# Recurrence of a hybrid transformer block on one core: the order of the next unit's transposes, its decay scan and its matmul bursts

## The chip, the core and the metric

The kernel runs on one core of a Trainium2 chip, in one launch. Five engines work side by side, each in the order of its own instruction queue: PE (matrix products, into PSUM), DVE (elementwise work), ACT (activations and copies), POOL (a few elementwise operations and some transfers) and SP (which here issues most of the DMA transfers). An instruction that waits for a semaphore holds everything behind it on its engine. The metric is the device time of one execution in microseconds; lower is better. One execution was recorded by the profiler.

## What is computed

One block with batch 1, 1024 tokens, width 1024. Two mixers read the same normalised input: an attention with a forget gate (8 heads of 64) and a linear recurrence of the RWKV-7 kind (8 heads of 64). Both are gated, added, projected, and followed by a convolutional feed-forward network. The recurrence, which is what the change touches:

```python
def step(state, inp):
    r_t, w_t, k_t, v_t, a_t, b_t = inp
    sa = jnp.einsum('bhvk,bhk->bhv', state, a_t)
    state = state * w_t[:, :, None, :] + sa[..., None] * b_t[:, :, None, :] \
        + v_t[..., None] * k_t[:, :, None, :]
    y_t = jnp.einsum('bhvk,bhk->bhv', state, r_t)
    return state, y_t
```

`w_t` is the decay `exp(-exp(w_log))`, and `a_t`, `b_t` come from the normalised key. The rest, in short:

```python
u = modulate(rms_norm(h, ln1_g), shift1, scale1)
p_fox, p_rwkv, p_gate = split(u @ w_in)
merged = sigmoid(gate_fox) * (o_fox @ fox_w_out) + sigmoid(gate_rwkv) * (o_rwkv @ rwkv_w_out)
h = h + gate1 * (merged @ w_o)
h = h + gate2 * conv_ffn(modulate(rms_norm(h, ln2_g), shift2, scale2))
return rms_norm(h, final_g)
```

## The kernel before

**Stages.** Load and normalise the input; small projections; the recurrence (about 180 to 665 us of the recorded span); the attention (to about 876 us); the merge, the output projection and the feed-forward network. Large products are made with operands split in a high and a low part (`hi`, `lo`), each a 128x128 weight tile against 512 columns.

**Units of the recurrence.** The heads are taken in four pairs `p`, the tokens in two halves `hf` of 512: eight units, numbered `k`, in the order (0,0), (0,1), (1,0) and so on. A unit has 8 chunks of 64 tokens. Its work falls in two generators.

`pre(k, p, hf)` prepares a unit. On DVE the decay scan `cum` (line 728) runs over the loaded decays; ACT makes the exponentials `el` and `en` from it; DVE makes `ar` and `bk` (lines 744 to 760) out of them. The PE burst `p` (two times 16 small matmuls, `bk` against `ar`) gives the chunk matrices `E` (DVE, line 776). They go out to DRAM (`sm`) and come back in another layout (`M`, four loads). On DVE 31 steps of two instructions each (`t`, line 796, and `E`, line 798; here called the inverse) invert the 32x32 blocks; step `s` is 31-s columns wide. The result goes out again (`se`) and comes back as `TT`. Meanwhile PE does transposes `vt`, `at`, `tb` and the product `q`.

`main(k, p, hf)` runs a unit. DVE transposes the blocks of `TT` into `X` (two instructions, line 853), PE does the small products `xi` and `zi` that complete the inverse, then `uw` and `mz` with DVE copies `Wt`, `Zt`, `Mt` between them, and then the scan over the 8 chunks: at each chunk PE adds to `sp` and `yp`, and DVE makes the new state `S` from `sp` (line 916), which the next chunk's PE step needs. At the end come the group norm of the output (`mu`, `va`) and the write `d_orw`.

**What sets the order.** PE's order is written out by the class `Weave`, a planner with its own clock `now`, in ns. Each matmul adds a fixed cost to it. A generator that yields a number asks to be resumed that much later. `run` resumes whichever chain is due, spawned chains (0) ahead of `main` (1) ahead of `pre` (2); while none is due, `fill` emits the next matmuls of the large projections: q and k (`qk`), r, k and v of the next head pair (`ps_rkv`), attention's values (`v`), and 16 gates (`gt`), of 48 matmuls each. Gates that are left when the recurrence ends are emitted in the same way in the attention, into the one bank `rk_ps`. `ready` is the planned time at which `TT` is expected: `main` does not emit `xi` before it. DVE, ACT, POOL and SP are ordered in this stage by the framework's scheduler, which works from priorities and its own estimates; a manual dependency of the kind `NOSYNC` only forbids it to place one instruction of an engine ahead of another.

Of the kernel before, what the change touches and what calls it, by code (L numbers as in the profile page):

```python
# [12 lines left out]
ALU = mybir.AluOpType  # L13
# [22 lines left out]
NOSYNC = mybir.DependencyInfo(mybir.DependencyClass.NoSync, mybir.DependencyReason.DATA)  # L36
# [11 lines left out]
class Weave:  # L48
# [27 lines left out]
    def add(self, load, run):  # L76
        self.queue.append((load, run))

    def prefetch(self):
        while (self.first or self.queue) and len(self.loaded) < 1:  # L80
            load, run = (self.first or self.queue).popleft()
            self.loaded.append((load(), run))
# [30 lines left out]

        self.live.append([self.now + wait, 0, chain])

    def run(self, chains):

        self.live = [[self.now, 1 + i, g] for i, g in enumerate(chains)]
        while self.live:
            due = min((c for c in self.live if c[0] <= self.now), key=lambda c: (c[1], c[0]), default=None)  # L120
            if due is None:
                self.fill(min(c[0] for c in self.live))
                continue
            wait = next(due[2], None)
            if wait is None:
                self.live.remove(due)
            else:
                due[0] = self.now + max(wait, 0.0)
# [3 lines left out]
def hybrid_block(ctx: ExitStack, tc: tile.TileContext, a, out):  # L132
    nc = tc.nc
    weave = Weave()
    ctx.enter_context(tc.manual_schedule(engines={mybir.EngineType.PE}))

    def mm(o, lhsT, rhs, start, stop, more=False):

        weave.mm_cost(o, lhsT, rhs)
        nc.tensor.matmul(o, lhsT, rhs, start=start, stop=stop, skip_group_check=more)  # L140
# [8 lines left out]
    tt, stt, ts = nc.vector.tensor_tensor, nc.vector.scalar_tensor_tensor, nc.vector.tensor_scalar  # L149
# [19 lines left out]
    def C(name):  # L169
        o, k = CST[name]  # L170
        return cst[:, o : o + k] if o < NC1 else cst2[:, o - NC1 : o - NC1 + k]
# [163 lines left out]
    with ExitStack() as es:  # L335
# [26 lines left out]
        def rkv_items(p, hf):  # L362
            ts_ = {x: rkp.tile([128, NH], F32, tag=f"{x}{hf}", name=f"{x}{p}{hf}") for x in "rkv"}
            rkv[p, hf], got[p, hf] = [ts_[x] for x in "rkv"], 0

            def steps(w, x, t):
                if hf == 0:
                    last_col[p, x] = shp.tile([128, 1], F32, tag=f"pv{x}", name=f"pv{p}{x}")
                yield from shifted(w, t, hf, ts_[x], last_col[p, x], f"rkv{t}")
                got[p, hf] += 1  # L370

            for x, t in (("k", 4 + p), ("r", p), ("v", 8 + p)):
                yield (lambda t=t: w_in(12 + t)), (lambda w, x=x, t=t: steps(w, x, t))
# [322 lines left out]
            return ap.rearrange("p (c x) -> p c x", x=x)  # L696

        BKS = (slice(0, 2), slice(1, 3))
        state, units, passed = {}, {}, set()

        blk_r = rw.tile([128, 128], F32R, name="blk_r")
        nc.scalar.copy(blk_r, C("blk"))
# [9 lines left out]
        def pre(k, p, hf):  # L712
# [5 lines left out]
            def tmp(nm, w=NH, bufs=1, dt=F32):  # L718
                return rw.tile([128, w], dt, tag=nm, name=f"{nm}{n}", bufs=bufs)

            def chunk_tile(nm, bufs, *dims):
                return rw.tile([128, *dims], F32, tag=nm, name=f"{nm}{n}", bufs=bufs)

            cum = tmp("cum")
            nc.sync.dma_start(cum, d_lora[0, p, :, cs])
            al = tmp("al")
            nc.sync.dma_start(al, d_lora[1, p, :, cs])
            nc.vector.tensor_tensor_scan(cum, C("reset"), cum, initial=0.0, op0=ALU.mult, op1=ALU.add)
            el = chunk_tile("el", 1, NCU, CH + 1)
            nc.gpsimd.memset(el[:, :, 0:1], 1.0)  # L730
            nc.scalar.activation(el[:, :, 1:], c3(cum), AF.Exp, scale=-DEC)
# [25 lines left out]
            pcd = chunk_tile("pcd", 3, NCU)  # L757
# [28 lines left out]
            M32 = chunk_tile("M32", 1, 32, 32)  # L786
            for g in range(4):
                nc.sync.dma_start(M32[g * 32 : g * 32 + 32, :, :], sm.rearrange("h c b s t -> (h c b) s t"))
            ready = weave.now + (46000 if k == 0 else 38500)
            E32 = chunk_tile("E32", 1, 8, 32)  # L790
            nc.gpsimd.tensor_copy(E32, C("einit").rearrange("p (j t) -> p j t", t=32))
            t32 = tmp("t32", 256)
            for s in range(31):
                J, W = s // 4 + 1, 31 - s
                tv = t32[:, 0 : J * W].rearrange("p (j w) -> p j w", w=W)
                tt(tv, E32[:, 0:J, s : s + 1].to_broadcast([128, J, W]),  # L796
                   M32[:, s : s + 1, s + 1 : 32].to_broadcast([128, J, W]), op=ALU.mult)
                tt(E32[:, 0:J, s + 1 : 32], E32[:, 0:J, s + 1 : 32], tv, op=ALU.add)  # L798
            se = scr.tile([2, NCU, 2, 32, 32], F32, tag="se", name=f"se{n}")
            for g in range(4):  # L800
                nc.sync.dma_start(
# [2 lines left out]
            TT = chunk_tile("TT", 2, NCU, CH)  # L804
# [37 lines left out]
        def main(k, p, hf):  # L842
# [3 lines left out]
            pcd, ar, E, QA, TT, bon, UV = (o[k] for k in ("pcd", "ar", "E", "QA", "TT", "bon", "UV"))  # L846


            X = rw.tile([128, NCU, 32], F32, tag="X", name=f"X{n}", bufs=1)
            B0 = (slice(0, 32), slice(64, 96))  # L850
            B1 = (slice(32, 64), slice(96, 128))
            for h in range(2):
                nc.vector.transpose(X[B0[h], :, :], TT[B0[h], :, 0:32])
            yield max(0, o["ready"] - weave.now)
            xi = gen(f"xi{n}")
            for c in range(NCU):
# [39 lines left out]
            sp = py.tile([128, NCU, CH], F32, tag="sp", name=f"sp{n}")  # L896
            S0 = state.get(p)

            def fixed(c):

                alone = hf == 0 and c == 0
                for h in range(2):
                    mm(sp[HS[h], c, :], E[:, c, h, 2, :], UV[:, c, h, :], start=True, stop=alone)
                for h in range(2):
                    mm(yp[HS[h], c, :], UV[:, c, h, :], E[:, c, h, 1, :], start=True, stop=alone)
# [3 lines left out]
            for c in range(NCU):  # L909
                if S0 is not None:  # L910
                    for h in range(2):
                        mm(sp[HS[h], c, :], Mt[HS[h], c, :], S0[HS[h], :], start=False, stop=True)
                S1 = None
                if not (hf == 1 and c == NCU - 1):
                    S1 = rw.tile([128, CH], F32, tag="state", name=f"S{n}{c}", bufs=3)
                    ts(S1, sp[:, c, :], pcd[:, c : c + 1], None, op0=ALU.mult)
                if S0 is not None:
                    for h in range(2):
                        mm(yp[HS[h], c, :], S0[HS[h], :], Zt[HS[h], c, :], start=False, stop=True)
                if c + 1 < NCU:  # L920
                    yield 1150
                    fixed(c + 1)
                S0 = state[p] = S1
# [55 lines left out]
        def pre_chain():  # L979
            for k, (p, hf) in enumerate(order):  # L980
                while got[p, hf] < 3:
                    weave.step()
                yield from pre(k, p, hf)
                if p < 3:
                    weave.first.extend(rkv_items(p + 1, hf))
                yield 0

        def main_chain():
            for k, (p, hf) in enumerate(order):
                while (p, hf) not in units:  # L990
                    yield 200
                yield from main(k, p, hf)
                yield 0

        weave.run([main_chain(), pre_chain()])
    rk_st.close()


# [307 lines left out]
    for x in range(2):  # L1306
        for n in range(8):
            if x or n:
                k = 8 * x + n + 1
# [157 lines left out]
    due = []  # L1467
# [248 lines left out]
    units = [(k, j) for k in ORDER for j in range(NP)]  # L1716
# [265 lines left out]
```

## Time and profile before

| | us |
|---|---|
| median of 3 runs | 1717.37 |
| the runs | 1715.96, 1721.29, 1717.37 |
| span of the profiled execution | 1713.2 |
| mean granted PE clock over the span | 0.986 |

The profile records the span from the first to the last instruction of the profiled execution and no other time of it; the runs' median is 4.2 us above that span.

The views used: the page's summary; the waits by engine (who sat idle for whom, in total us, number of times, longest); the timeline (start, duration, engine, line, operation, output<-inputs, shapes, count, and in brackets the idle time just before with what ended it); windows (busy time of each engine in a stretch, then the granted PE clock as a share of full speed, the DMA engines' share and GB/s); the DMA issues with the time to landing. A few stretches of this kernel, from windows of 100 us:

| stretch, us | PE busy | DVE busy | PE clock |
|---|---|---|---|
| 200 to 300 | 96.89 | 80.56 | 0.98 |
| 300 to 400 | 96.66 | 75.15 | 1.00 |
| 400 to 500 | 95.28 | 72.56 | 0.98 |
| 500 to 600 | 96.54 | 70.52 | 0.98 |
| 600 to 700 | 96.21 | 37.38 | 0.98 |
| 800 to 900 | 94.70 | 79.34 | 1.00 |
| 1000 to 1100 | 99.98 | 58.14 | 1.00 |

### The profile page before, as it was taken

Reading aid. Unit: us, or ns where it says so; the run is one execution under the profiler, and the core shown is the slowest. Engines: PE = TensorE matmul, PEld = TensorE weight load, DVE = VectorE, ACT = ScalarE, POOL = GpSimd, SP = SyncE. Lnnn points to the kernel's source line nnn. Section 1 sums busy time; section 2 is a strip of 40 time slices with the busy share of each in tenths; the row PEclk is TensorE's granted clock in tenths of the full one; section 3 lists DMA queues with packets and bytes.
Section 4 is the critical chain, followed back from the end, with each engine's and each line's share of the span. In section 5 each row is a group of like instructions: output and inputs, shape, how many; then the busy total and the mean of one; then the engine's idle time right before and its main releaser. Section 6 shows DMA issues by size and latency. Waiting matters only on the chain.

```text
span 1713.2 us, 26506 instructions
## 1 busy us (share of the span) xinstructions
PE 1665.3 (97%) x9984; PEld 1367.0 (80%) x9984; DVE 1213.0 (71%) x2432; ACT 813.1 (47%) x1482; POOL 143.5 (8%) x175
## 2 busy tenths in 40 slices
PE   8899999999999999999999999999999999999998
PEld 7867777787777777888878888888888888888886
DVE  4576687777677632889777734897777777786677
ACT  5364343334344454766652314664444444454455
POOL 0001011111110002323212100000000000000000
PEclk9899999999999999999999999999999999999999
DMA  9287644533333226434268611132333223484463
GB/s 310 89 304 236 185 133 112 140 96 116 95 96 98 85 81 158 135 100 125 75 231 288 255 50 62 57 105 98 106 116 111 93 99 117 149 293 153 123 215 111
DMA packets 135311, 239.87 MB, mean 140 GB/s; under 512 B 39888, under 2 KB 64720, under 8 KB 135184
## 3 DMA queue, kind: packets, MB, share of 16 engines
q1 hardware_dynamic: 127232, 220.94, 39.8%
q0 software_dynamic: 7952, 17.25, 3.7%
q8 instruction: 78, 1.28, 0.3%
q14 instruction: 49, 0.40, 0.1%
HBM read 172.59 MB, written 65.54 MB: 139 GB/s over the span
## 4 chain that ended last, share of the span: by engine, by line
PE 80%; DVE 9%; DMA 4%; ACT 3%; SPq 2%; issue 1%; DVEq 0%; ACTq 0%; POOLq 0%
PE X L140 13%; PE D L140 12%; PE Y L140 6%; PE wo L140 5%; PE gt L140 5%; PE br L140 5%; PE ps_rkv L140 5%; PE qk L140 4%; PE rk_ps L140 4%; PE W L140 3%; PE lg L140 2%; PE ov L140 2%; PE tr L140 2%; PE sp L140 2%; PE tp L144 2%
## 5 line engine op out<-in xcount | busy, mean ns | idle before, releaser
L140 PE MATMUL D<-op,op 128*128 128x512 f32 x924 | 209.8, 389 | 0.0
L140 PEld LDWEIGHTS D<-op,op 128*128 128x128 f32 x924 | 173.3, 188 | 36.3 <-DVE op L1245 0.3
L140 PE MATMUL X<-T_m,S 128*128 128x512 f32 x440 | 107.3, 390 | 0.1
L140 PEld LDWEIGHTS X<-T_m,S 128*128 128x128 f32 x440 | 82.4, 188 | 18.2 <-ACT T_m L1670 0.6
L1244 ACT CAST op<-g 128x512 fp32r<-128x512 f32 x77 | 47.8, 621 | 73.0 <-PE D L140 47.9
L1245 DVE TENSOR_TENSOR op<-g,op 128x512 fp32r<-128x512 f32 x77 | 53.0, 689 | 40.9 <-ACT op L1244 40.8
L1481 DVE SCALAR_TENSOR_TENSOR c<-ab,vec,c 128x512 f32<-128x512 f32 x88 | 65.9, 749 | 19.5 <-ACT c L1484 17.9
L263 DVE TENSOR_TENSOR lo_in<-raw_in,hi_in 128x512 fp32r<-128x512 f32 x84 | 56.4, 706 | 31.6 <-PE gt L140 12.3
L796 DVE TENSOR_TENSOR t<-E,M 128x60 f32<-128x60 f32 (+24 forms) x248 | 56.8, 229 | 29.5 <-DMA M<-sm 24.2
L1445 DVE TENSOR_TENSOR S<-ur,S 128x512 fp32r<-128x512 f32 x66 | 45.5, 691 | 35.6 <-ACT S L1441 35.5
L261 ACT CAST hi_in<-raw_in 128x1024 fp32r<-128x1024 f32 x42 | 43.9, 1047 | 52.5 <-PE ps_rkv L140 17.2
L1441 ACT CAST S<-ur 128x512 fp32r<-128x512 f32 x66 | 41.0, 622 | 55.6 <-DVE ur L1434 30.6
L1445 DVE TENSOR_TENSOR A<-ur,A 128x512 fp32r<-128x512 f32 x64 | 44.0, 688 | 30.9 <-ACT A L1441 30.7
L140 PE MATMUL Y<-T_h,A 128*128 128x512 f32 x264 | 63.5, 389 | 0.0
L140 PE MATMUL Y<-T_h,S 128*128 128x512 f32 x264 | 63.3, 389 | 0.0
L140 PE MATMUL X<-B_b,A 128*128 128x512 f32 x252 | 60.8, 390 | 0.0
L140 PE MATMUL W<-B_f,A 128*128 128x512 f32 x252 | 60.6, 389 | 0.0
L1066 ACT ACTIVATE P<-lg,nm 128x896 f32<-128x896 f32 (+3 forms) x64 | 47.5, 744 | 22.1 <-DVE nm L1062 21.9
L140 PEld LDWEIGHTS Y<-T_h,A 128*128 128x128 f32 x264 | 49.6, 188 | 10.4
L798 DVE TENSOR_TENSOR E<-E,t 128x60 f32<-128x60 f32 (+24 forms) x248 | 53.7, 216 | 5.8
L140 PEld LDWEIGHTS Y<-T_h,S 128*128 128x128 f32 x264 | 49.5, 188 | 10.3
L1441 ACT CAST A<-ur 128x512 fp32r<-128x512 f32 x64 | 39.9, 623 | 34.2 <-PE X L140 31.5
(472 smaller groups left out, 4213.3 us busy)
## 6 DMA issues: line engine op xcount, KB each, us to landing
raw_in<-in_w_in SPq DMA_DIRECT2D x50, 512.0 KB, 3.7
wm<-in_w_mod SPq DMA_DIRECT2D x48, 512.0 KB, 6.5
ur<-in_w_up SPq DMA_DIRECT2D x44, 512.0 KB, 4.0
g<-d_g SPq DMA_DIRECT2D x35, 512.0 KB, 3.9
d_g<-gs SPq DMA_DIRECT2D x44, 256.0 KB, 2.0
d_g<-c SPq DMA_DIRECT2D x33, 256.0 KB, 4.4
d_st<-qh SPq DMA_DIRECT2D x64, 128.0 KB, 2.4
d_gate<-gs SPq DMA_DIRECT2D x32, 256.0 KB, 2.6
```

What stands on the lines that cost most here:

```text
L140: nc.tensor.matmul(o, lhsT, rhs, start=start, stop=stop, skip_group_check=more)
L144: nc.tensor.transpose(o, i, eye)
L261: nc.scalar.copy(hi, raw)
L263: nc.vector.tensor_tensor(lo[:, c : c + NH], raw[:, c : c + NH], f32(hi[:, c : c + NH]), op=ALU.subtract)
L796: tt(tv, E32[:, 0:J, s : s + 1].to_broadcast([128, J, W]), M32[:, s : s + 1, s + 1 : 32].to_broadcast([128, J, W]), op=ALU.mult)
L798: tt(E32[:, 0:J, s + 1 : 32], E32[:, 0:J, s + 1 : 32], tv, op=ALU.add)
L1066: nc.scalar.activation(e[:, 0:n], lg[:, 0:n], AF.Exp, bias=nm[:, 0:1], accum_out=nm[:, 1:2])
L1244: nc.scalar.copy(hi, src)
L1245: tt(lo, src, f32(hi), op=ALU.subtract)
L1441: nc.scalar.copy(hi, src)
L1445: tt(lo, src, f32(hi), op=ALU.subtract)
L1481: stt(c, ab[:, x + hf * NH : x + hf * NH + NH], V("conv_w", 22 * x + i), c, op0=ALU.mult, op1=ALU.add)
```

## The change

It has four parts, all in the recurrence. (1) From the second unit on, the decay scan `cum` may not stand on DVE ahead of step 22 of the inverse of the unit before. (2) From the second unit on, the transposes `X` may not stand on DVE ahead of the last state `S` of the unit before. (3) The first unit's planned `ready` is 6000 ns later. (4) `run` gets `beside` (2600 ns): when a `pre` burst is due, and the next `main` step or spawned chain falls due within 2600 ns, PE is filled up to that step, the step is emitted first, and the burst right behind it.

```diff
-    def run(self, chains):
+    def run(self, chains, beside=0.0):
 
         self.live = [[self.now, 1 + i, g] for i, g in enumerate(chains)]
+        led = False
         while self.live:
             due = min((c for c in self.live if c[0] <= self.now), key=lambda c: (c[1], c[0]), default=None)
-            if due is None:
-                self.fill(min(c[0] for c in self.live))
+            lead = min((c[0] for c in self.live if c[1] < 2), default=None)
+            if due is None or (due[1] > 1 and not led and lead is not None and lead < self.now + beside):
+                self.fill(min(c[0] for c in self.live) if due is None else lead)
+                led = False
                 continue
+            led = beside > 0 and (led or due[1] < 2)
             wait = next(due[2], None)
...
-        state, units, passed = {}, {}, set()
+        state, units, passed, placed = {}, {}, set(), {}
...
-            nc.vector.tensor_tensor_scan(cum, C("reset"), cum, initial=0.0, op0=ALU.mult, op1=ALU.add)
+            i = nc.vector.tensor_tensor_scan(cum, C("reset"), cum, initial=0.0, op0=ALU.mult, op1=ALU.add)
+            if k:
+                tc.add_manual_dep(i.ins, placed["inverse"].ins.name, NOSYNC)
...
-            ready = weave.now + (46000 if k == 0 else 38500)
+            ready = weave.now + (52000 if k == 0 else 38500)
...
-                tt(E32[:, 0:J, s + 1 : 32], E32[:, 0:J, s + 1 : 32], tv, op=ALU.add)
+                i = tt(E32[:, 0:J, s + 1 : 32], E32[:, 0:J, s + 1 : 32], tv, op=ALU.add)
+                if s == 22:
+                    placed["inverse"] = i
...
-                nc.vector.transpose(X[B0[h], :, :], TT[B0[h], :, 0:32])
+                i = nc.vector.transpose(X[B0[h], :, :], TT[B0[h], :, 0:32])
+                if k:
+                    tc.add_manual_dep(i.ins, placed["state"].ins.name, NOSYNC)
...
-                    ts(S1, sp[:, c, :], pcd[:, c : c + 1], None, op0=ALU.mult)
+                    placed["state"] = ts(S1, sp[:, c, :], pcd[:, c : c + 1], None, op0=ALU.mult)
...
-        weave.run([main_chain(), pre_chain()])
+        weave.run([main_chain(), pre_chain()], beside=2600.0)
```

What it does to the engines' orders shows at three places. In the names, the digits behind a tile's name are its unit's half (and the chunk, for `S_11`: half 1, chunk 1) and a buffer number; line numbers of the changed kernel are a few higher.

First, DVE while the first unit (0,0) is being inverted and the second, (0,1), prepared. Before:

```order
L384 SCALAR_TENSOR_TENSOR ql_1_1811<-qk_1_1718,qh_1_1809 128x512
L728 SCALAR_TENSOR_TENSOR cum_1_1792<-cst_120,cum_1_1792 128x512
L798 TENSOR_TENSOR E_0_1607<-E_0_1607,t_0_1609 128x3x23
L796 TENSOR_TENSOR t_0_1609<-E_0_1607,M_0_1602 128x66
L798 TENSOR_TENSOR E_0_1607<-E_0_1607,t_0_1609 128x3x22
L753 TENSOR_TENSOR ar_1_1856<-r_748,el_1_1797 128x512
```

Now:

```order
L267 TENSOR_TENSOR lo_in_1923<-raw_in_1920,hi_in_1922 128x512 x2
L802 TENSOR_TENSOR t_0_1609<-E_0_1607,M_0_1602 128x54
L388 SCALAR_TENSOR_TENSOR ql_1_1912<-qk_1_1885,qh_1_1910 128x512
L804 TENSOR_TENSOR E_0_1607<-E_0_1607,t_0_1609 128x6x9
L732 SCALAR_TENSOR_TENSOR cum_1_1792<-cst_120,cum_1_1792 128x512
L802 TENSOR_TENSOR t_0_1609<-E_0_1607,M_0_1602 128x48
L804 TENSOR_TENSOR E_0_1607<-E_0_1607,t_0_1609 128x6x8
L802 TENSOR_TENSOR t_0_1609<-E_0_1607,M_0_1602 128x49
L804 TENSOR_TENSOR E_0_1607<-E_0_1607,t_0_1609 128x7x7
L755 SCALAR_TENSOR_TENSOR ar_1_1856<-kr_1_1853,nkk,el_1_1797 128x512
```

The scan of (0,1) stood behind the inverse's step 7 (the `E` of 2x24 is some rows above it, that of 3x23 right behind it) and now stands behind step 22 (`E` of 6x9); 29 instructions of the inverse have moved ahead of it. PE's order is the same in both kernels up to and past the burst `p` of (0,1).

Second, DVE in the scan of unit (1,1), with the transposes of (2,0). Before:

```order
L916 TENSOR_SCALAR S_11_4469<-sp_1_4401,pcd_1_3030 128x64
L750 SCALAR_TENSOR_TENSOR kr_1_4411<-kr_1_4411,vec,al_1_4323 128x512
L853 STREAM_TRANSPOSE X_0_4862<-TT_0_4032 32x256
L751 TENSOR_TENSOR bk_1_4413<-kr_1_4411,en_1_4329 128x8x64
L754 TENSOR_SCALAR al_1_4323<-al_1_4323,vec,oka 128x512
L853 STREAM_TRANSPOSE X_0_4862<-TT_0_4032 32x256
L916 TENSOR_SCALAR S_12_4485<-sp_1_4401,pcd_1_3030 128x64
```

Now (all states of the scan stand above these rows):

```order
L804 TENSOR_TENSOR E_0_4143<-E_0_4143,t_0_4145 128x8
L782 TENSOR_TENSOR E_1_4716<-p_2_100_4719,cst_120 128x4x128
L782 TENSOR_TENSOR E_1_4716<-p_2_110_4720,cst_120 128x4x128
L267 TENSOR_TENSOR lo_in_4108<-raw_in_4105,hi_in_4107 128x512 x2
L267 TENSOR_TENSOR lo_in_4748<-raw_in_4745,hi_in_4747 128x512 x2
L861 STREAM_TRANSPOSE X_0_4928<-TT_0_4213 32x256
L978 TENSOR_TENSOR vs_7_4741<-v_7_4686,vs_7_4741 128x4x64
L861 STREAM_TRANSPOSE X_0_4928<-TT_0_4213 32x256
```

The two transposes no longer stand between two states; they stand behind the first half of the next unit's `E`.

Third, PE where the recurrence ends and the attention begins. Before:

```order
L140 MATMUL va_1_6960<-Zts_1_6961,blk_r 128x512
L140 MATMUL va_1_6960<-Mts_1_6962,blk_r 128x512
L140 MATMUL gt_1_6975<-u_lo,hi_in_6792 128x512 x3
L140 MATMUL gt_1_6975<-u_hi,lo_in_6793 128x512 x8
L140 MATMUL rk_ps<-u_hi,hi_in_6928 128x512 x8
L140 MATMUL rk_ps<-u_lo,hi_in_6928 128x512 x8
L140 MATMUL rk_ps<-u_hi,lo_in_6929 128x512 x8
```

Now:

```order
L144 MATMUL va_1_6988<-Zts_1_6989,blk_r 128x512
L144 MATMUL va_1_6988<-Mts_1_6990,blk_r 128x512
L144 MATMUL gt_0_7014<-u_lo,hi_in_6903 128x512 x7
L144 MATMUL gt_0_7014<-u_hi,lo_in_6904 128x512 x8
L144 MATMUL gt_1_7090<-u_hi,hi_in_6903 128x512 x8
L144 MATMUL gt_1_7090<-u_lo,hi_in_6903 128x512 x8
L144 MATMUL gt_1_7090<-u_hi,lo_in_6904 128x512 x8
L144 MATMUL rk_ps<-u_hi,hi_in_7009 128x512 x8
```

One more gate (48 matmuls) is emitted in the recurrence: 10 there and 6 in the attention, where it was 9 and 7. From the last head sums `va` to the attention's first gate there were 11 matmuls and are 39. In the attention the gate matmuls that are missing are those of its last part.

## Prediction

> **What bounds the kernel now.** I read the page's summary first:
>
> ```profile
> span 1713.2 us, 26506 instructions
> PE 1665.3 (97%) x9984; PEld 1367.0 (80%) x9984; DVE 1213.0 (71%) x2432; ACT 813.1 (47%) x1482; POOL 143.5 (8%) x175
> ```
>
> PE is busy for 97% of the span, and the change leaves the set of matmuls as it is: they only change places. So the time can move only by PE's idle time and by stretches in which PE runs at a lower granted clock. The waits of PE say for whom it idles (us in total, times, longest):
>
> ```profile
> PE sp L140 <- DVE S L916: 8.3, 6, 2.5
> ...
> PE rk_ps L140 <- ACT gm L1167: 3.7, 2, 3.5
> ...
> PE xi L140 <- DVE X L853: 3.1, 2, 1.8
> ...
> PE ps_rkv L140 <- DVE k L358: 1.4, 1, 1.4
> PE at L144 <- DVE E L776: 1.1, 1, 1.1
> ```
>
> In the recurrence that is 8.3+3.1+1.4+1.1 = 13.9 us. DVE's timeline shows what DVE stood on just before; the bracket is its own idle time:
>
> ```profile
> 241.70 0.43 DVE L853 STREAM_TRANSPOSE X<-TT 32x256 f32<-32x256 f32 x1 [5.01 <-DMA TT<-se]
> 305.24 1.23 DVE L728 TENSOR_TENSOR_SCAN cum<-cst,cum 128x512 f32<-128x512 f32 x1 [2.10 <-DMA cum<-d_lora]
> 405.21 1.22 DVE L728 TENSOR_TENSOR_SCAN cum<-cst,cum 128x512 f32<-128x512 f32 x1 [2.61 <-DMA cum<-d_lora]
> 432.80 0.43 DVE L853 STREAM_TRANSPOSE X<-TT 32x256 f32<-32x256 f32 x1 [2.79 <-DMA TT<-se]
> 500.07 0.43 DVE L853 STREAM_TRANSPOSE X<-TT 32x256 f32<-32x256 f32 x1 [4.37 <-DMA TT<-se]
> 542.98 0.43 DVE L853 STREAM_TRANSPOSE X<-TT 32x256 f32<-32x256 f32 x1 [3.04 <-DMA TT<-se]
> ```
>
> Each time DVE stands in front of a scan or a transpose whose data has not landed, and a state `S` that is ready to be made waits behind it. PE then stands at `sp`, as in these two:
>
> ```profile
> 435.11 0.34 PE L140 MATMUL sp<-UV,E 128*64 128x64 f32 x4 [2.45 <-DVE S L916]
> 544.30 0.34 PE L140 MATMUL sp<-UV,E 128*64 128x64 f32 x4 [2.23 <-DVE S L916]
> ```
>
> And behind three of the stalls the granted clock (the column after POOL) halves:
>
> ```profile
> 244.50:247.90 3.40, 3.40 (x9) 2.75 (x9) 3.02 (x13) 1.83 (x4) 0.19 (x1) 0.50 0.45 147
> 435.70:439.10 3.40, 3.40 (x18) 2.24 (x16) 2.04 (x4) 0.57 (x1) 0.00 (x0) 0.50 0.20 69
> 544.90:548.30 3.40, 3.40 (x20) 2.24 (x18) 3.13 (x6) 1.25 (x2) 0.00 (x0) 0.50 0.22 80
> ```
>
> Each of these windows is 3.4 us at half speed, so about 1.7 us of work is lost in it, 5.1 in all.
>
> **The stalls that go.** The second part forbids `X` ahead of the last `S`, so the stalls at 435.11 and 544.30 and the one behind 500.07 lose their cause; the first part does the same for `cum` at 305.24 and 405.21. The first unit's transposes (241.70) have no state to wait for. There PE itself stands at `xi` (3.1 us in the waits); the third part lets it do 6 us of other matmuls first, which covers it. Of the 13.9 us I put 0.7 down to ordinary late states that have no such wait on DVE in front: 13.2 go, and with the clock 13.2+5.1 = **-18.3 us**. The bounds are -13.2, if the half-clock windows come anyway, and -18.3.
>
> **The stall that comes.** In the first overlap, unit (0,1) being prepared, DVE has no wait on `cum` that would be worth removing, yet the scan goes behind step 22 of the inverse there too. PE's order is the same up to the burst `p`. Before:
>
> ```profile
> 201.21 0.19 DVE L796 TENSOR_TENSOR t<-E,M 128x31 f32<-128x31 f32 x1 [5.65 <-DMA M<-sm]
> 207.75 1.21 DVE L728 TENSOR_TENSOR_SCAN cum<-cst,cum 128x512 f32<-128x512 f32 x1
> 210.78 0.22 DVE L796 TENSOR_TENSOR t<-E,M 128x60 f32<-128x60 f32 x1
> 211.04 0.22 DVE L798 TENSOR_TENSOR E<-E,t 128x60 f32<-128x60 f32 x1
> 214.72 0.69 DVE L751 TENSOR_TENSOR bk<-kr,en 128x512 f32<-128x512 f32 x1
> 216.66 0.68 DVE L756 TENSOR_TENSOR bk<-al,en 128x512 f32<-128x512 f32 x1
> 218.06 1.28 DVE L263 TENSOR_TENSOR lo_in<-raw_in,hi_in 128x512 fp32r<-128x512 f32 x2
> 219.27 0.68 DVE L384 SCALAR_TENSOR_TENSOR ql<-qk,qh 128x512 fp32r<-128x512 f32 x1
> 218.08 1.16 PE L140 MATMUL p<-ar,bk 64*128 64x128 f32 x16
> ```
>
> The last `bk` ends at 216.66+0.68 = 217.34, and `p` starts at 218.08: there is less than 1 us of slack. Now 29 instructions of the inverse go ahead of `cum`. One takes 0.26 us with its gap (210.78 to 211.04): 7.5 us. With them two `ql`, the pair `lo_in` and one `kr` go ahead: 0.6+0.6+1.2+0.6 (each counted 0.6 because the next starts before the 0.68 are over, as at 218.06 to 219.27, 1.21 for two), less 0.4 of overlap: 10.1 together, so `cum` starts at 217.9 and not 207.75. Behind it come the scan 1.2, four more of the inverse 1.0, seven operations that make `ar` and `bk` (seven times about 0.6 = 4.2) and four more of the inverse that overlap them partly, 0.6. The last `bk` is done at 217.9+1.2+1.0+4.2+0.6 = 224.9. PE stands at `p` from 218.08, for 6.9 us, with all its matmuls and weight loads queued behind. The inverse cannot start earlier to make room: at 201.21 DVE had already idled 5.65 us for `M`. Stalls a third as long were followed by half clock above, so I add 1.3 of the 1.7 (part of that window may fall into the stall itself): **+8.2 us**. The bounds are 6 (overlap as close as it gets, no clock) and 10.
>
> **The later odd units.** When (1,0), (2,0) and (3,0) are inverted, `main` of the unit before runs its scan, and now `cum` and two `lo` fall between two states.
>
> ```profile
> 269.21 0.33 PE L140 MATMUL sp<-S,Mt 64*64 64x64 f32 x4
> 271.56 0.33 PE L140 MATMUL sp<-S,Mt 64*64 64x64 f32 x4
> 283.98 1.29 DVE L776 TENSOR_TENSOR E<-p,cst 128x512 f32<-128x512 f32 x2
> 293.01 0.52 DVE L796 TENSOR_TENSOR t<-E,M 128x31 f32<-128x31 f32 x1 [3.52 <-DMA M<-sm]
> ```
>
> PE offers a chunk every 271.56-269.21 = 2.35 us; of that DVE may be about 1.85 late before PE idles (an estimate: 2.35 less the state's own 0.3 and a hand-over). Counted from the start of the even unit's `p`: its two halves with 16 fills of about 0.23 between them and `E` behind, 7.5 us; from there to the landing of `M` 293.01-(283.98+1.29) = 7.7; then 44 inverse instructions to step 22 and the dozen wider ones between them, 17.3 us. The state of chunk 1 comes at 32.5 us, where PE would offer it at about 31: inside the slack. To the state of chunk 2 DVE has `cum` 1.1, two `lo` 1.2 and five of the inverse 1.2, which makes 3.6 where 2.35 are at hand: about 1 us of stall in each of three units. **+3 us**, bounds 0 and 3 x (3+1.7) = 14; I take the near end because the sum lands inside the slack.
>
> **At the attention's front** the first gate waits:
>
> ```profile
> 668.35 1.98 PE L140 MATMUL rk_ps<-u_hi,hi_in 128*128 128x512 f32 x8
> 670.16 1.98 PE L140 MATMUL rk_ps<-u_lo,hi_in 128*128 128x512 f32 x8
> 676.28 0.60 ACT L1166 ACTIVATE gs<-rk_ps 128x512 f32<-128x512 f32 x1 [4.42 <-DMA d_gate<-gs]
> 677.42 3.32 PE L140 MATMUL rk_ps<-u_hi,hi_in 128*128 128x512 f32 x8 [3.47 <-ACT gm L1167]
> d_gate<-gs SPq DMA_DIRECT2D x4, 256.0 KB, 8.6
> 678.00:681.40 3.40, 3.40 (x10) 2.63 (x8) 0.69 (x1) 1.18 (x2) 0.00 (x0) 0.50 0.97 257
> ```
>
> ACT waits for an earlier gate's write, which takes 8.6 us beside the other loads, and PE for ACT: 3.47 and 1.7 of clock. Now 39 instead of 11 matmuls stand between `va` and this gate, 28 x 0.226 (670.16-668.35 = 1.81 for eight) = 6.3 us, more than the 4.42. What is left is the 1.14 us that ACT needs to empty the bank (676.28 to 677.42) and some clock: **-3.5 us**, bounds -5.2 and 0.
>
> **At its end** a gate of 48 matmuls, 48 x 0.226 = 10.9 us, is missing:
>
> ```profile
> 842.40:875.60 33.20, 30.14 (x187) 25.95 (x185) 24.44 (x50) 22.97 (x52) 0.00 (x0) 1.00 0.11 39
> ```
>
> Of the 33.2 us PE's own work fills 30.14 with that gate and about 19.3 without; DVE needs 24.4 there. PE already idles 3.1 of this stretch. The work that was moved is lost as cover where DVE then bounds: 33.2-10.9 = 22.3 is below 24.4, so at least 2.1 are lost, at most all 10.9. The kernel's rows hold nothing between; ACT and DVE are both short of the whole stretch, which is nearer to the low end: **+5 us**.
>
> The bursts right behind a scan step cost nothing: the same matmuls in another place, with the fills that were there now ahead of the step. `xi` and `zi` now follow each other without fills, behind `tb` and `q` of the next unit, which take longer than ACT's copies between them; the cost without this cover is at most 1 us in each of six units, which is in the range.
>
> **Sum:** -18.3+8.2+3-3.5+5 = -5.6 us, against the span of 1713.2, thus 1707.6. The median of the runs lies 4.2 above the span, so the forecast is 1717.4-5.6 = **1711.8**. A measurement of this kernel can tell about 0.3% from no change: below 1712.2 is faster, above 1722.5 slower.
>
> **Rivals.** *The stall at `p` is hidden* (the scheduler's order overlaps more than I count): -5.6-8.2 is -13.8, 1703.5. For it: 217.34 to 218.08 is slack. Against: DVE has no idle time between 201 and 218. Chance 0.15, faster.
>
> *DVE falls behind in the odd units.* If the state of chunk 1 itself comes over 1.85 us late, each of three units stalls about 3 us more and falls to half clock, and with DVE's later rows as dense as the cadence nothing is caught up: 3 x (3+1.7) = 14 in place of 3, so -5.6+11 = +5.4, 1722.8, and more where a further state is late. For it: the sum had only 0.3 us to spare. Against: DVE was busy for 70 to 75% of these hundreds of microseconds. Chance 0.20: slower 0.17, same 0.03.
>
> *What is won is given back in the attention*: its end loses all 10.9 and the front's stall stays, -5.6+5.9+3.5 = +3.8, 1721.2. For it: the write at the front still competes with loads. Chance 0.07, same 0.05, slower 0.02.
>
> *The half clock is not the short stalls' doing.* The windows at 435.7 and 544.9 come 0.6 us behind stalls of 2.45 and 2.23 us; if they come for another reason, 5.1 stay: 1716.9. Chance 0.03, same. The Trainium skill, "TensorE: Matmul & The Clock Gate", in "Why this matters for your kernels", speaks for it: it says that throughput drops when PE idles for more than about 3 us. By that rule these two stalls should have cost no clock. The trace shows half clock behind both, so I go with the trace.
>
> **Chances.** The forecast has 0.55, its own range 1705 to 1717: it lies at the border, so faster 0.33, same 0.21, slower 0.01. With the rivals: faster 0.33+0.15 = 0.48; same 0.21+0.03+0.05+0.03 = 0.32; slower 0.01+0.17+0.02 = 0.20. The range reaches over the hidden stall and the odd units: 1702 to 1724.
>
> **What would show it.** Right: DVE no longer waits at `X` or `cum` between two states; `sp` waits for `S` in total 3 us or less; PE has one idle stretch of about 7 us at `p` near 218; `rk_ps` waits about 1; PE idles 5 us more in the last 30 us of the attention. I am wrong if the idle stretch at `p` is under 4 us, if `sp` still waits for `S` over 8 us in total, or if half-clock windows appear that no stall precedes.

## The result and the profile after

The changed kernel takes 1725.12 us (median of 15 runs, 1720.01 to 1732.09) against 1717.37 (15 runs, 1711.49 to 1721.29): a ratio of 1.0046, 95% interval 1.0032 to 1.0061. It is slower by about 8 us, where 5.6 us less were forecast, and lies just above the range. The profiled execution of the changed kernel is one of 1725.12 us, with a span of 1723.0.

The page's summary and the waits of PE in the changed kernel (us in total, times, longest):

```profile
span 1723.0 us, 26533 instructions
...
PE 1668.1 (97%) x9984; PEld 1373.0 (80%) x9984; DVE 1219.8 (71%) x2434; ACT 814.7 (47%) x1481; POOL 139.2 (8%) x170
```

```profile
PE rk_ps L144 <- ACT gm L1177: 8.1, 2, 7.9
PE p L144 <- DVE bk L762: 7.0, 2, 6.5
...
PE sp L144 <- DVE S L926: 3.8, 4, 1.2
PE uw L144 <- ACT TT L877: 3.3, 2, 2.1
...
PE ps_rkv L144 <- DVE t L802: 1.7, 1, 1.7
```

`sp` fell from 8.3 to 3.8, and `xi` (3.1) and `at` (1.1) are gone. In their place `p` rose from 0.7 to 7.0 and `rk_ps` from 3.7 to 8.1, and there is a new wait, `uw` for `TT`. Windows by stage show where it counts (length, then busy us of PE, PEld, DVE, ACT and POOL, granted clock, DMA share, GB/s). First the kernel before, then the changed one; the stages are the first overlap, the first unit's run, the rest of the recurrence, the attention's front and its last 34 us:

```profile
180.00:236.00 56.00, 55.31 (x371) 44.52 (x370) 44.02 (x116) 23.03 (x38) 7.48 (x8) 1.00 0.63 172
236.00:302.00 66.00, 62.89 (x603) 48.50 (x602) 49.07 (x150) 23.97 (x43) 7.58 (x13) 0.97 0.44 119
302.00:666.00 364.00, 352.47 (x3308) 281.47 (x3308) 237.46 (x692) 162.60 (x285) 40.95 (x54) 0.99 0.34 100
666.00:692.00 26.00, 22.21 (x96) 17.67 (x95) 10.33 (x19) 12.41 (x24) 10.74 (x13) 0.93 0.78 184
843.00:877.64 34.64, 29.64 (x183) 25.70 (x183) 24.83 (x50) 23.93 (x54) 0.00 (x0) 1.00 0.15 52
```

```profile
180.00:236.00 56.00, 48.91 (x291) 39.18 (x290) 40.26 (x109) 19.05 (x31) 4.71 (x7) 0.91 0.63 165
236.00:302.00 66.00, 65.84 (x545) 51.52 (x544) 45.30 (x130) 25.67 (x44) 7.83 (x11) 1.00 0.43 115
302.00:666.40 364.40, 355.68 (x3466) 287.00 (x3465) 252.15 (x721) 168.37 (x296) 44.87 (x59) 1.00 0.35 102
666.40:700.00 33.60, 25.61 (x104) 20.37 (x102) 7.55 (x11) 11.53 (x20) 6.59 (x10) 0.85 0.72 181
853.00:887.30 34.30, 26.23 (x150) 22.13 (x148) 25.50 (x54) 21.65 (x51) 0.00 (x0) 0.90 0.11 37
```

PE's idle time in a stage is the length less the busy time. To it comes half of the time that PE was busy at half clock, which the record of the granted clock gives. Together they are what the stage lost:

| stage | before: idle, busy at half clock, lost | after | difference |
|---|---|---|---|
| up to 180 us | 12.69, 19.01, 22.2 | 12.27, 16.56, 20.6 | -1.6 |
| first overlap | 0.69, 0, 0.7 | 7.09, 5.88, 10.0 | +9.3 |
| first unit's run | 3.11, 3.41, 4.8 | 0.16, 0, 0.2 | -4.6 |
| rest of the recurrence | 11.53, 6.82, 14.9 | 8.72, 0, 8.7 | -6.2 |
| attention's front | 3.79, 3.41, 5.5 | 7.99, 5.81, 10.9 | +5.4 |
| attention's middle | 3.40, 3.41, 5.1 | 2.87, 6.17, 6.0 | +0.9 |
| attention's last 34 us | 5.00, 0, 5.0 | 8.07, 6.82, 11.5 | +6.5 |
| the rest | 7.64, 6.83, 11.1 | 7.76, 6.83, 11.2 | +0.1 |

The differences add up to about +9.7, and the two spans differ by 9.8. These are single executions: e8 below has the order of the kernel before on every engine, and its trace loses 3.3 us more in the rest of the recurrence. So a difference of a few us in one stage is not a cause by itself. The stall at `p` came as forecast:

```profile
217.37 1.22 DVE L732 TENSOR_TENSOR_SCAN cum<-cst,cum 128x512 f32<-128x512 f32 x1
...
223.50 0.69 DVE L762 TENSOR_TENSOR bk<-al,en 128x512 f32<-128x512 f32 x1
```

```profile
224.34 2.04 PE L144 MATMUL p<-ar,bk 64*128 64x128 f32 x15 [6.54 <-DVE bk L762]
```

`cum` starts at 217.37 (the working said 217.9), and the last `bk` ends at 224.19 (224.9). The attention's front did not come as forecast. ACT's timeline there, PE's, POOL's in the kernel before and in the changed one, and the piece of the chain of waits behind it (start, duration, what):

```profile
678.52 0.60 ACT L330 ACTIVATE gs<-gt 128x512 f32<-128x512 f32 x1 [5.33 <-DMA d_gate<-gs]
687.48 0.60 ACT L1176 ACTIVATE gs<-rk_ps 128x512 f32<-128x512 f32 x1 [5.64 <-DMA d_gate<-gs]
```

```profile
688.62 3.78 PE L144 MATMUL rk_ps<-u_hi,hi_in 128*128 128x512 f32 x8 [7.90 <-ACT gm L1177]
```

```profile
662.64 0.76 POOL L1008 DMA_DIRECT2D stA<-d_st  x1
...
666.77 1.04 POOL L255 CAST hi_in<-raw_in 128x1024 fp32r<-128x1024 f32 x1 [1.81 <-PE gt L140]
667.75 0.70 POOL L1008 DMA_DIRECT2D stA<-d_st  x1
```

```profile
662.79 0.75 POOL L1018 DMA_DIRECT2D stA<-d_st  x1
...
665.09 0.72 POOL L1018 DMA_DIRECT2D stA<-d_st  x1
```

```profile
673.23 14.18 DMA d_gate<-gs
```

Two gates in a row now wait for a write, and the write issued at 673.23 takes 14.18 us. The second head's loads are issued at 665.09, 2.3 us behind the first head's. In the kernel before, 5.1 us and a cast (`hi_in`, 666.77) lay between them. The gates of the recurrence and of the attention share one pair of buffers (tag `sp0`), so a gate cannot be made before the write of the gate two places ahead has landed.

### The profile page after: what moved, and what is told of

It reads as the page before. It is cut to its first block, busy times and chain, and to the rows that moved or that the text cites. A ratio compares the mean times of both kernels' runs of the same rounds, so it can differ in the third digit from the quotient of the medians.

```text
span 1723.0 us, 26533 instructions
## 1 busy us (share of the span) xinstructions
PE 1668.1 (97%) x9984; PEld 1373.0 (80%) x9984; DVE 1219.8 (71%) x2434; ACT 814.7 (47%) x1481; POOL 139.2 (8%) x170
## 4 chain that ended last, share of the span: by engine, by line
PE 60%; DVE 5%; ACT 2%; DMA 1%; issue 1%; SPq 0%; DVEq 0%; ACTq 0%
PE X L144 13%; PE D L144 12%; PE Y L144 6%; PE wo L144 5%; PE br L144 5%; PE gt L144 4%; PE rk_ps L144 3%; PE W L144 3%; PE lg L144 2%; PE ov L144 2%; PE tp L148 2%; PE tr L144 1%; DMA d_gate<-gs 1%; DVE P L1082 1%; DVE nm L1072 1%
## 5 line engine op out<-in xcount | busy, mean ns | idle before, releaser
L1072 DVE TENSOR_REDUCE nm<-lg 128x1 f32<-128x896 f32 (+3 forms) x64 | 46.8, 752 | 13.4 <-PE lg L144 12.5
```

Source lines behind the costliest of these rows:

```text
L1072: nc.vector.tensor_reduce(nm[:, 0:1], lg[:, 0:n], axis=AX.X, op=ALU.max, negate=True)
```

## The experiments

Each is timed in 6 to 15 runs against the kernel before on the same chip; not all were on one chip, so kernels are compared with one another by their ratios. The table gives the parts of the change in each kernel and the ratio with its 95% interval. "Scan from (1,0)" means the first part from the third unit on (`k > 1`).

| run | parts | ratio |
|---|---|---|
| the change | 1, 2, 3, 4 | 1.0046 (1.0032 to 1.0061) |
| e1 | scan from (1,0), 2, 3, 4 | 1.0009 (0.9995 to 1.0023) |
| e2 | the change, own gate buffer | 1.0013 (1.0000 to 1.0026) |
| e3 | the change, second head's loads behind the cast | 1.0010 (0.9997 to 1.0024) |
| e4 | 1, 2, 3 | 1.0007 (0.9995 to 1.0019) |
| e5 | e1 with own gate buffer | 1.0015 (1.0002 to 1.0027) |
| e6 | e11 with own gate buffer | 1.0004 (0.9990 to 1.0019) |
| e7 | 2 | 0.9973 (0.9960 to 0.9987) |
| e8 | none, own gate buffer | 1.0020 (1.0005 to 1.0035) |
| e9 | scan from (1,0), 2 | 0.9927 (0.9913 to 0.9942) |
| e10 | 1, 2, 4 | 1.0005 (0.9994 to 1.0015) |
| e11 | scan from (1,0), 2, 3 | 0.9993 (0.9982 to 1.0004) |
| e12 | e9 with `ready` at 49000 | 0.9935 (0.9920 to 0.9950) |
| e13 | scan from (1,0), 2, 4 | 0.9975 (0.9966 to 0.9985) |
| e14 | 1, 2 | 0.9967 (0.9958 to 0.9976) |

e9, e14, e11, e13, e4, e10, e1 and the change are the eight combinations of three pieces on top of e9: the scan's order in the second unit, the third part and the fourth. Each piece alone costs: 0.40% (e14), 0.66% (e11) and 0.48% (e13). Taken out of the whole change, each gives back 0.37% (e1), 0.41% (e10) and 0.39% (e4). So no single one of them is what made the change slower.

**e1: the scan from the third unit on.**

```diff
-            if k:
+            if k > 1:
                 tc.add_manual_dep(i.ins, placed["inverse"].ins.name, NOSYNC)
```

> The changed kernel with the order on the decay scan only from the third unit on (k > 1), so the scan of (0,1) is again ahead of most of the inverse of (0,0); PE's order is the same. Theory (the balance of the two traces): the idle stretch of 6.5 us at the burst p near 218 and the half clock behind it go, 9.4 us less than the changed kernel, so about 1.5 us below the kernel before (ratio 0.999); every other wait of PE stays as in the changed kernel, that of the attention's first gate at 7.9 us too. Rival (the stall only shifts the work against the transfers): what is saved at p comes back as longer waits for M, TT or the gate writes later, and the time stays within 3 us of the changed kernel, ratio 1.003 or more.

It fell by 0.37% (1.0046 to 1.0009), about 6 us, and the stall at `p` is gone from the trace. The rest of the 9.4 came back, as the rival has it in part: a wait of 2.8 us at `qk` for `v` near 240, and `uw` for `TT` rose from 3.3 to 5.3 us, with a half-clock stretch of 6.8 us that begins within the longer one. One wait did not stay as the theory has it: that of the attention's first gate, 7.9 us in the changed kernel, is 3.7 in e1.

**e2: a buffer of its own for the attention's gates, and e3: the second head's loads behind the cast.**

```diff
-            g = gsp.tile([128, NH], F32, tag="sp0", name=f"gs{i}_{hf}")
+            g = at.tile([128, NH], F32, tag="gl", name=f"gs{i}_{hf}", bufs=1)
```

```diff
             i = nc.gpsimd.tensor_copy(hi, raw)
+            marks.setdefault("late", i)
...
+        if h == 1:
+            for z in (x, y, i):
+                tc.add_manual_dep(z.ins, marks["late"].ins.name, NOSYNC)
```

(`x`, `y` and `i` are the loads of `stA`, `stB` and `vh`.)

> The changed kernel with a buffer of its own for the gates made in the attention, in place of the two that they share with the recurrence's gates; the order of every engine is the same. Theory: at the attention's front PE waits because that buffer is held until an earlier gate's write has landed; with its own buffer the wait of rk_ps falls from 7.9 us to under 1 us and the half clock behind it goes: 8 to 10 us below the changed kernel, ratio to the kernel before about 0.999. Rival (the transfers themselves are the bound, the two heads' loads and the gate's weights): the wait only moves to the next matmul that needs a loaded tile, and the time falls by under 3 us, ratio 1.003 or more.

> The changed kernel with the three loads of the second head placed on POOL behind the cast of the gate's weights, where they stood in the kernel before; all other engines' orders are the same. Theory: in the changed kernel both heads' loads are issued back to back near 663 to 667 us and fill the DMA engines, so the gate writes issued at 667.7 and 673.2 land only near 678 and 687; with the cast between them the first write lands in under 5 us, ACT no longer waits 5.3 us for it, and the wait of rk_ps falls from 7.9 to between 0 and 4 us: 4 to 9 us below the changed kernel. Rival (the second write is late whatever stands in front of the first): the wait of rk_ps stays over 6 us and the time within 2 us of the changed kernel.

PE at the first gate in e2, then ACT and PE in e3:

```profile
686.55 2.11 PE L144 MATMUL rk_ps<-u_hi,hi_in 128*128 128x512 f32 x8 [2.21 <-ACT gm L1177]
```

```profile
678.34 0.60 ACT L331 ACTIVATE gs<-gt 128x512 f32<-128x512 f32 x1 [4.07 <-DMA d_gate<-gs]
683.03 0.60 ACT L1180 ACTIVATE gs<-rk_ps 128x512 f32<-128x512 f32 x1 [1.38 <-DMA d_gate<-gs]
```

```profile
684.17 2.14 PE L144 MATMUL rk_ps<-u_hi,hi_in 128*128 128x512 f32 x8 [2.38 <-ACT gm L1181]
```

Either edit takes the wait from 7.90 to about 2.3 us and the kernel down by 0.33 to 0.36%. The instructions' order is the same in e2, and in e3 only POOL's differs. So e2 shows the shared buffer as a cause of the wait, and e3's runs show that the loads' place costs time in this kernel. In e3 it went another way than its theory had it: the first of the two gates still waits 4.07 us (5.33 before), and it is the second write that lands sooner (5.64 to 1.38).

That the write is late because the two heads' loads stand together is not shown. In e1 they stand together too, and around the front PE, ACT, POOL and SP have the order of the changed kernel; yet ACT and PE wait less there:

```profile
681.33 0.60 ACT L1176 ACTIVATE gs<-rk_ps 128x512 f32<-128x512 f32 x1 [1.91 <-DMA d_gate<-gs]
682.46 3.64 PE L144 MATMUL rk_ps<-u_hi,hi_in 128*128 128x512 f32 x8 [3.72 <-ACT gm L1177]
```

The second write, which takes 14.18 us in the changed kernel, takes 10.00 in e1 (issued at 671.24). In e13 the cast stands between the two heads' loads, and the write issued at 663.36 still takes 12.60 us and PE waits 6.6. What sets the time of this write stays open.

**e4: without the fourth part, and e10: without the third.**

```diff
-        weave.run([main_chain(), pre_chain()], beside=2600.0)
+        weave.run([main_chain(), pre_chain()])
```

```diff
-            ready = weave.now + (52000 if k == 0 else 38500)
+            ready = weave.now + (46000 if k == 0 else 38500)
```

> The changed kernel without its fourth part (bursts right behind due scan steps); the first three parts stay. POOL's order at the attention's front is then that of the kernel before, and 15 instead of 39 matmuls stand between va and the attention's first gate; the gate that moved into the recurrence stays moved. Theory (part four brought the front's stall by moving the loads together, the third part moved the gate and so cost the attention's tail): p's stall stays at 6.5 us, the wait of rk_ps falls to 3 to 4 us as before the change, the attention's tail keeps its loss: 3 to 7 us below the changed kernel, ratio 1.001 to 1.003. Rival (the moved gate, not the loads' place, makes the front's stall): the wait of rk_ps stays over 6 us, ratio 1.004 or more.

> The changed kernel without its third part (the first unit's planned landing of TT back at 46000). Seven gates are then left for the attention as before the change, in place of six. Theory (the gate that moved costs the attention's front and tail): the front's wait of 7.9 us falls to about 4, the tail's loss of 7.6 us in the balance falls to 2 to 4, while the stall of 6.5 us at p stays: ratio 1.000 to 1.002. Rival (front and tail lose for other reasons than the moved gate): within 2 us of the changed kernel, ratio 1.0035 or more.

Both ratios are close to what the theories gave, and far from the rivals'. Their waits at the first gate, 5.6 and 5.9 us, are not: they were expected at 3 to 4. So the front's wait is not made by one part alone, and the parts do not settle it either: e1 has the third and the fourth and shows 3.7. In e10 seven gates are left for the attention, and its last part is as in the kernel before.

**e5, e6, e8: the own buffer in other company.** The edit is that of e2, on e1, on e11 and on the kernel before.

> The changed kernel with both the scan's order from the third unit on only and the own buffer of the attention's gates. Alone they brought the changed kernel (ratio 1.0046 to the kernel before) to 1.0009 and 1.0013. Theory (two separate losses): the gains add, 0.37% and 0.33%, ratio about 0.9975, and the first gate's rk_ps waits about 2 us. Rival (both only give PE's lost time back to the same later waits, uw for TT and the first gate): the gains overlap, ratio 0.999 or more.

> As the run before, and without the fourth part (bursts right behind due scan steps). Theory: without that part the waits of uw for TT (3.3 us in the changed kernel, 5.3 where the scan was moved) are not there, but two of about 1.6 us of at for E are; the stall of 6.5 us at p is gone and the first gate's wait of 5.6 us falls below 2: 8 to 13 us below the changed kernel without its fourth part (ratio 1.0007), that is 0.993 to 0.996. Rival (the fourth part is what wins in this combination): ratio 0.998 or more.

> The kernel before with the own buffer of the attention's gates and nothing of the change. Theory: the first gate's wait of 3.5 us goes with its half-clock window, 4 to 5 us, ratio 0.997 to 0.9975. Rival (in the kernel before that wait is not the buffer's but the transfers'): within 2 us of the kernel before, ratio 0.999 or more.

All three theories failed: e5 and e6 came out where their rivals put them, and e8 even above its rival. In e8 the timelines of ACT and PE show part of the reason:

```profile
675.44 0.60 ACT L1166 ACTIVATE gs<-rk_ps 128x512 f32<-128x512 f32 x1 [2.12 <-PE rk_ps L140]
...
688.23 0.60 ACT L1166 ACTIVATE gs<-rk_ps 128x512 f32<-128x512 f32 x1 [3.56 <-DMA d_gate<-gs]
```

```profile
689.46 0.76 PE L140 MATMUL rk_ps<-u_hi,hi_in 128*128 128x512 f32 x1 [3.79 <-ACT gm L1167]
```

The first gate no longer waits for a write, but the single buffer makes the second one wait 3.56 us for the first one's. The wait moved by one gate. A pair of own buffers was not tried. e8's trace loses 1.9 us more at the front; the 3.3 us more in the recurrence come at the same order and have no explanation here. Why e5 is not below e1 isn't settled: its first gate waits 2.2 us, against 3.7 in e1, and the attention's last part has more half-clock windows.

**e7, e9: the second part alone, and with the scan from the third unit on.** PE's order is that of the kernel before in both.

> The kernel before with the second part alone: the transposes X stand behind the last state of the unit before; PE's order is that of the kernel before. Theory (what the prediction counts for this part): the waits of sp at 435 and 544 (2.45 and 2.23) and of at at 501 (1.08) go with two half-clock windows of 1.7 each, 9 us, ratio 0.995. Rival (the transposes are then late themselves, and the gain comes back as a wait of xi for X or at for E): ratio 0.998 or more.

> The kernel before with the second part (transposes behind the last state) and the first part from the third unit on (scan behind step 22); PE's order is that of the kernel before. Theory: to what the transposes gave alone (ratio 0.9973) the scan adds the waits that it made at sp near 310 (2.4 us) and at ps_rkv near 405 (1.4), less about 1 us each where the scan now stands between two states: 0.9955 to 0.9965. Rival (behind step 22 the scan holds up the states of the odd units as much as it did before by waiting): 0.997 to 0.999.

e7 wins 0.27%, half of the theory: the waits at `sp` near 435 and 544 are gone, but that of `at` for `E` rose from 1.1 to 3.1. e9 wins 0.73%, more than expected, 1704.15 us (median of 6), and is the fastest kernel of the study. What PE waits for in the recurrence of e9:

```profile
PE xi L144 <- DVE X L861: 3.1, 2, 1.8
PE sp L144 <- DVE S L926: 2.6, 4, 1.0
```

The states' 8.3 us have become 2.6, and of the three half-clock windows in the recurrence only the one at `xi` is left.

**e11, e12: the third part on top of e9, whole and halved.**

> As the first run of this call and with the third part too (planned landing 6000 ns later, so one gate more in the recurrence and six left for the attention). Theory: the first unit's two waits of xi (3.1 us and a half-clock window, 4.8) go, and 2.8 us at qk for v come in their place; the moved gate costs the first gate's wait 2 us and the attention's tail 3 to 5: 3 to 5 us above the first run, ratio 0.998 to 0.999. Rival (the moved gate costs nothing): equal to the first run or below.

> As the first run of this call with the planned landing 3000 ns later instead of 6000, which leaves seven gates for the attention as in the kernel before. Theory: half of the first unit's waits of xi is covered (3.1 us to under 1.5, the half-clock window may go) and the attention keeps its cover: 2 to 4 us below the first run, ratio about 0.994. Rival (what is covered at xi comes back as the wait of qk for v, 2.8 us): within 1 us of the first run.

At 49000 seven gates stay for the attention, at 52000 six. The first costs nothing that can be told (0.9935 against 0.9927), the second 0.66%, some 11 us, where the theory had 3 to 5. Most of that is the moved gate: beside e9's trace, that of e11 loses 6.6 us more in the stretch below and 2.1 more at the front, by the sum of the section above. Another 2.4 lie before 180 us, where nothing was changed. The last 35 us of the attention in e9, then in e11:

```profile
830.00:864.60 34.60, 29.68 (x183) 25.75 (x183) 24.76 (x50) 23.84 (x54) 0.00 (x0) 0.99 0.15 52
```

```profile
843.00:877.90 34.90, 26.72 (x153) 22.50 (x151) 25.92 (x55) 21.94 (x51) 0.00 (x0) 0.90 0.11 38
```

The stretch is as long with the gate as without it. PE has 30 matmuls less in it, idles 8.2 us in place of 4.9 and runs two windows at half clock, though neither DVE nor ACT is busy for more than three quarters of it. The chain of waits through it in e11 passes from DVE to PE to ACT, and no line has more than 13.2% of it: PE's gates only filled a chain from engine to engine. The other half of the theory of e11 and the rival of e12 are seen in DVE and PE of e11:

```profile
241.60 0.43 DVE L861 STREAM_TRANSPOSE X<-TT 32x256 f32<-32x256 f32 x1 [5.03 <-DMA TT<-se]
...
243.70 0.75 DVE L362 SCALAR_TENSOR_TENSOR v<-ps_rkv,omu,sh_rkv 128x512 f32<-128x512 f32 x1
```

```profile
244.51 0.79 PE L144 MATMUL qk<-u_hi,hi_in 128*128 128x512 f32 x1 [2.74 <-DVE v L362]
```

DVE still stands at `X` for `TT`, and behind it stands `v`, which empties the PSUM bank that PE's other matmuls need. PE does not wait at `xi` any more, it waits at `qk`.

**e13, e14: the fourth part alone on e9, and the scan's order in the second unit alone.**

> Second part, first part from the third unit on, and the fourth part (bursts right behind due scan steps); the third part is left out, so seven gates stay for the attention; 30 instead of 11 matmuls stand between va and its first gate. Theory (the fourth part makes waits of its own in the recurrence: states of the odd units later, uw for TT behind a gate's operation, 5 us more idle than without it): 3 to 7 us above the kernel without the fourth part (ratio 0.9927), 0.9945 to 0.9965. Rival (it costs only together with the moved gate): 0.992 to 0.9935.

> Second part, and the first part from the second unit on as in the changed kernel; third and fourth part left out. Theory: the stall of 6.5 us at p near 218 with half clock behind it comes, less the first unit's wait of xi (3.1 us and its half-clock window, 4.8) that goes because PE arrives there later: 4 to 6 us above the kernel without it (ratio 0.9927), 0.995 to 0.9965. Rival (the stall's whole 9.4 us stays, nothing is covered): 0.998 or more.

Both went the way of their theories, at a higher price: e13 is 0.48% above e9, some 8 us where 3 to 7 were expected, and e14 0.40%, 7 us where 4 to 6 were. In e14 the waits of PE show the stall at `p` and none at `xi`:

```profile
PE p L144 <- DVE bk L762: 6.8, 2, 6.5
```

So in the changed kernel the late `p` alone makes `xi` late enough, without the third part. In e13 new waits come with the bursts behind the scan steps, the longest at `uw` (DVE, ACT and PE):

```profile
506.86 0.19 DVE L802 TENSOR_TENSOR t<-E,M 128x31 f32<-128x31 f32 x1 [7.76 <-DMA M<-sm]
507.31 0.69 DVE L333 SCALAR_TENSOR_TENSOR gs<-gt,gs 128x512 f32<-128x512 f32 x1
```

```profile
508.03 0.63 ACT L334 ACTIVATE gs<-gs 128x512 f32<-128x512 f32 x1 [4.30 <-DVE gs L333]
508.57 0.73 ACT L877 COPY TT<-zi 32x256 f32<-32x256 f32 x2
```

```profile
508.97 1.30 PE L144 MATMUL uw<-QA,TT 64*64 64x128 f32 x14 [3.53 <-ACT TT L877]
```

DVE stands at the inverse's first step for `M`; a gate's `gs` waits behind it; ACT waits for `gs`, with the copy of `TT` behind; PE waits for `TT`. It is the kind of wait that the change removes at `X` and `cum`, at another place. The first gate's wait is 6.6 us in e13 against 3.9 in e9.

## Why the prediction was wrong

The working of the parts that the change is about came out right as a sum. The prediction put the transposes and the scan from the third unit on at -18.3 less the 4.8 of `xi`, and +3 in the odd units, -10.5 us; e9 measured 0.73%, 12.5, and its trace loses 10.4 us less than the kernel before in the rest of the recurrence. That this sum came so close is partly luck, because its pieces did not: the transposes alone, put at 9 us, gave 0.27% (e7, 4.6 us), and the scan's order on top of them 0.46%, some 8 us, where e9's theory had 1 to 3. It put the scan in the second unit at +8.2. The trace lost 9.3 in that stage (6.5 of standing at `p` where 6.9 were counted, and 2.9 by the half clock where 1.3 were), and e14 lost 0.40%, 7 us, after the gain at `xi`.

Between the forecast of -5.6 and the +9.8 of the two spans lie 15.4 us. The attention's front makes 8.9 of them, the recurrence behind the first overlap 4.5, the attention's end 1.5 and `p` 1.1; the other stages take back 0.6. The steps that failed are those in which a piece of the change was costed by what it covers and not by what it carries along.

- **The attention's front, -3.5 us.** "Now 39 instead of 11 matmuls stand between `va` and this gate ... more than the 4.42." It lost 5.4 us more in place of 3.5 less, the largest error of the sum. The 28 matmuls belong to a gate, and that gate has a write of its own, which needs the buffer pair and is in turn waited for: ACT stands for 5.33 us and then for 5.64, and PE for 7.90. e2 shows the buffer's part in it. The second head's loads had also lost the cast that stood between them and the first head's on POOL, where the prediction did not look, and e3's runs show that their place costs time. Why the write takes as long as it does, 14.18 us here and 10.00 in e1, is open.
- **The first unit's `xi`, covered by "6 us of other matmuls".** e11 and e12 show 2.7 us at `qk` in its place. In the changed kernel the stage is clean (0.2 us lost), but because of the stall at `p`, as e14 shows without the third part. The third part thus gains nothing and moves the gate: it costs 0.66% in e11, and without it the change is 0.41% faster (e10).
- **The attention's end, +5 us.** That a missing gate is lost as cover was right. It lost 6.5: 3.1 of idle time and 3.4 by the two half-clock windows of the last 34 us, which were not counted. That DVE bounds there is not shown; it is busy for 25.50 of 34.30 us.
- **The bursts right behind a scan step, nothing.** "The same matmuls in another place" holds for PE, not for what waits for them: 0.48% in e13, and 0.39% between e4 and the change. Part of it stands in the changed kernel as `uw` 3.3 us and `ps_rkv` 1.7, so the recurrence won 10.8 us (4.6+6.2) and not 18.3-3 = 15.3.

Smaller slips change nothing in this. Behind the waits at 405 and 500 it was not a state `S` that waited: PE stood there for `k` (at `ps_rkv`) and for `E` (at `at`). And 1.1+1.2+1.2 is 3.5 and not 3.6, 1717.4-13.8 is 1703.6 and not 1703.5.

Of the rivals, "what is won is given back in the attention" comes nearest to what happened, with a price that was too low. It had the end lose all 10.9 (6.5 measured) and the front's stall stay as it was; the stall more than doubled. The half-clock windows did go with the stalls at `sp`: there is none between 302 and 666 us in the changed kernel.

## What to carry to other kernels

When a change of order shifts filler work from one stage to another, list what each shifted piece brings with it (here a buffer and a write) and who waits for it there; the time that the piece itself takes is not its whole cost. An order rule that pays in most rounds of a loop should not be applied in the round in which nothing was late: here that round gave back more than half of the gain. And a number in a planner that is moved by a few microseconds can tip a whole unit of work over a stage's border, so the counts per stage are to be compared before the time. Last, before a wait in one trace is given a cause, look for a run with the same order at that place: e1 has the front of the changed kernel and less than half of its wait.

## What had not been expected of the hardware

The half clock does not need a long gap. Idle pieces of 1.0, 1.5 and 1.1 us between 861 and 876 us in the changed kernel were each too short for one window, yet windows of 3.41 us at half clock stand at 868.5 and 878.8. And the stall of 6.5 us at `p` was followed by half clock for 10.24 us in four traces (the change, e2, e10, e14) and for 6.83 us in two (e3, e4). Where it is longer it begins earlier, within the stall, so PE was busy at half clock for 5.3 to 6.4 us in all six and lost 2.7 to 3.2 us. The prediction had 1.3 there. All these lengths (3.41, 6.83, 10.24) are multiples of 3.41 us. The Trainium skill, "TensorE: Matmul & The Clock Gate", section "What's actually happening", speaks of a free-running window of 3413 ns. The traces agree with that length. The advice of its section "Why this matters for your kernels", to avoid gaps over about 3 us, does not cover gaps like these.
